# Hybrid attention block on one core: DMA additions to x moved behind the accumulations of weights, and the last additions written ahead of the rows

## The chip, the core and the metric

The kernel runs on one core of a Trainium2 chip. The metric is the device time of one execution in microseconds (us). Before the change three executions took 796.5, 797.93 and 798.8 us; the median, 797.93 us, is what a changed kernel is compared with.

## What is computed

One layer, float32, on 512 rows of 2048 numbers: a normalised sliding-window attention with 32 query and 4 key heads whose output is gated and multiplied by `w_out`, then a gated addition of an embedding, then a last normalisation.

```python
hn = rmsnorm(x, norm_g)
x = x + swa_mixer(hn, w_in, w_out, sinks, rel_bias)
emb = p @ ple_proj
g = sigmoid(rmsnorm(x, ple_norm) @ ple_gate)
x = x + emb * g
return rmsnorm(x, final_g)
```

The change lies in the last three lines.

## The kernel before, in words

**Products.** Every float32 matrix is split into a high part (a rounded copy, made by ACT, L755 or L763) and a low part (the rest, made by DVE, L756 or L764), and a product is three matmuls (`mm3`, L123). The big products by `w_out` and `ple_gate` follow a scheme with seven products of quarter matrices in place of eight, one level of it again for some of them. The products are numbered 1, 7, 6, 5, 3, 4 (`ORDER_PLE`). Each number p has two halves jj = 0, 1 of 512 columns; such a half is called the unit (p, jj) here. `unit` (L992) takes four pieces of weights, m = 0 to 3, and each piece, written (p, jj, m), is 128x1024 numbers (512 KB) and feeds 12 matmuls. Product 4 of the second matrix is no unit: it is done at the end in four blocks (`block`, L1568; jj, row block tb): (0,0), (1,0), (0,1) and (1,1), the last of them cut into a lower and an upper part.

**Weights.** `Pieces` (L720) hands them out. `get` of a piece first makes the loads and the splits that are due: a piece is split two pieces ahead of its use and loaded four raw pieces ahead. Loads go out on SP's queue (L747). Raw tiles (`braw`) have four buffers, so that a load waits for the split of the piece four before; the high and low tiles have three, so that a split waits for the matmuls of the piece three before. For products 7, 6 and 4 the weights are one sum that grows in place: loaded once for 7 (`grown`), then 6's and 4's share is added to it by an accumulating DMA on POOL's queue (L734), which must wait until the split for the product before has read the tile. There are eight such accumulations for 6 and eight for 4. The eight pieces of product 4 are split by `split_last(k)` (L759) at the steps that `early` (L1468) names, k = 7 at the very end.

**Gated additions.** `gated` (L1381) adds e * sigmoid(product) to one 128x512 tile of x, in steps: a sigmoid (ACT, L1387), a product with e (DVE, L1389) and the addition itself, then the square with its sum for the last normalisation (ACT, L1404). The addition is an accumulating DMA on POOL's queue (L1391, 256 KB) where rows and columns are both in the first or both in the second half, and a DVE instruction (L1393) elsewhere. Called "sum", for the first quarter of x (rows 0 to 255, columns 0 to 1023), there are four such DMAs; product 5 has four, for the last quarter; product 3 and the blocks of 4 use DVE.

**The order written out.** From the second product of `ORDER_PLE` on nothing is scheduled by a planner: each engine runs its instructions in the order in which the program writes them. `later` is a list of steps, and after each piece `some_later(4 - m)` (L987) runs a share of it so that it is empty by the last piece of a unit; then `todo` (L1513) makes loads of e (L1371), a step of the next product's left operands (`fh` on ACT and `fl` on DVE, L865 and L866), `split_last`, `open_bank` (L1473) and `by_gain` (L1413, multiplication of a finished tile by `final_g`). `gate_later` (L1455) puts the steps of a gate in front of `later`. For "sum" and for product 5 it keeps the squares apart in `moved`; they are put on `later` at the end of the units (5,0) and (5,1), and what is left over is run among the blocks. The loads of e are SP instructions in the same order.

**The end.** After the units, `power_of_mean` (L1355) makes the factor of the last normalisation, `row` (L1419) and ACT multiplications make the finished rows, `store` (L1416) writes them, for rows 0 to 255 first (`rows_out`, L1424), then 256 to 383, then the last.

Of the kernel before, what the change touches and what calls it, by code (L numbers as in the profile page):

```python
# [55 lines left out]
def trunk_kernel(ctx: ExitStack, tc: tile.TileContext, a: dict):  # L56
# [101 lines left out]
    def run(gen):  # L158
        for _ in gen:
            pass  # L160
# [21 lines left out]
    kinds, g = [], 0  # L182
# [16 lines left out]
    for k in range(KC):  # L199
# [95 lines left out]
        if 3 <= k < 3 + NB:  # L295
            t = k - 3
# [384 lines left out]
    def block(nm, r, c, jj, m):  # L681

        r = r if nm == "w_out" else 3 - r
        return a[nm][2 * (c - 1) + jj, 4 * (r - 1) + m]
# [16 lines left out]
    for nm, p in SUMS:  # L701
        for q in (6, 5) if (nm, p) == ("ple_gate", 5) else (p,):
            sum_small(nm, q)
        for jj in range(2):
            for m in range(4):
                t = summed[nm, p, jj, m] = tc.dram_tile([P, WE], F32, name=f"{nm}_{p}_{jj}_{m}")
# [278 lines left out]
    later = []  # L985
# [369 lines left out]
    def power_of_mean(out, ssq, nm):  # L1355

        w = out.shape[-1]
        ms = const.tile([P, NB], F32, tag="ms_r", name=f"ms_{nm}")[:, :w]
        nc.vector.tensor_scalar(ms, ssq, 1.0 / D, EPS, op0=ALU.mult, op1=ALU.add)
        yield  # L1360
        nc.gpsimd.tensor_tensor(out, ms, power[:, :w], op=ALU.pow)
# [7 lines left out]
    def load_embeds(c, jj):  # L1369
        t = embed_of[c, jj] = late.tile([P, 2, 512], F32, tag="e", name=f"e{c}_{jj}", bufs=2)  # L1370
        nc.sync.dma_start(t, embeds[c, jj])  # L1371
# [9 lines left out]
    def gated(t, j, zin, z, e, c=slice(0, 512), share=1.0):  # L1381


        n = done[t]
        done[t] += 1
        xt = x1[j][:, t, c]
        nc.scalar.activation(z, zin, AF.Sigmoid, scale=rstd2[:, t : t + 1])  # L1387
        yield
        nc.vector.tensor_mul(z, e[:, c], z)  # L1389
        if (t >= 2) == (j >= 2):  # L1390
            nc.gpsimd.dma_start(xt, z, accum_op=ALU.add)  # L1391
        else:
            nc.vector.tensor_add(xt, xt, z)  # L1393
        yield
        if (t, j) == (3, 1) and share != 1.0:
            flat = x1s.rearrange("p j t c -> p (j t c)")
            at = (NB + 3) * 512
            xt = flat[:, at + c.start : at + c.stop + 1]
            nc.vector.scalar_tensor_tensor(
                out=s2[:, 1, 1, c.start - 1 : c.stop], in0=xt, scalar=share, in1=xt, op0=ALU.mult, op1=ALU.mult,  # L1400
                accum_out=ssq3[:, t, n : n + 1],
            )
        elif (t, j) != (3, 1):
            nc.scalar.activation(z, xt, AF.Square, accum_out=ssq3[:, t, n : n + 1])  # L1404
        else:
            nc.vector.scalar_tensor_tensor(
                out=z, in0=xt, scalar=share, in1=xt, op0=ALU.mult, op1=ALU.mult, accum_out=ssq3[:, t, n : n + 1]
            )

    def gain(j):  # L1410
        return fg[:, j * 512 : (j + 1) * 512]

    def by_gain(t, j):  # L1413
        nc.vector.tensor_mul(x1[j][:, t, :], x1[j][:, t, :], gain(j))

    def store(t, j):  # L1416
        nc.sync.dma_start(a["out"][t * P : (t + 1) * P, j * 512 : (j + 1) * 512], x1[j][:, t, :])

    def row(t, j, yn):  # L1419

        xt = x1[j][:, t, :]
        nc.vector.scalar_tensor_tensor(out=xt, in0=xt, scalar=yn, in1=gain(j), op0=ALU.mult, op1=ALU.mult)

    def rows_out(t):  # L1424

        for j in (2, 3):
            row(t, j, yn2[:, t : t + 1])
            store(t, j)
        for j in range(2):
            nc.scalar.mul(x1[j][:, t, :], x1[j][:, t, :], yn2[:, t : t + 1])  # L1430
            store(t, j)
# [3 lines left out]
    def gate(p, jj, ps, e):  # L1435

        zs = []
        for tb in range(2):
            v1, v2, v7 = s1[:, jj, tb], s2[:, jj, tb], s7[:, jj, tb]
            if p == 1:  # L1440
                nc.scalar.mul(v1, ps[tb], -1.0)
            elif p == 7:
                (nc.vector.tensor_copy if tb else nc.scalar.copy)(v7, ps[tb])
            elif p == 6:
                nc.vector.tensor_add(v2, ps[tb], v7)
            elif p == 5:
                nc.vector.tensor_add(v7, ps[tb], v7)
                zs.append((2 + tb, 2 + jj, v7, v7))
            elif p == 3:
                zs.append((tb, 2 + jj, ps[tb], v1))  # L1450
            else:
                zs.append((tb, jj, v1, v1))
        return [gated(*z, e[z[0]]) for z in zs]

    def gate_later(*v):  # L1455
        zs = gate(*v)
        steps = [[partial_of(next, z, None) for z in zs] for _ in range(3)]
        if v[0] in (5, "sum"):
            moved.append(steps.pop())
        later[:0] = [step for of in steps for step in of]  # L1460


    moved = []

# [11 lines left out]
    opens = {  # L1478
        (3, 1, 0): (0, 0, "t"), (3, 1, 1): (1, 0, "t"), (3, 1, 2): (0, 1, "o"), (3, 1, 3): (1, 1, "o", lower),
    }  # L1480
    gains = {(3, 0, 1): (0, 0), (3, 0, 2): (1, 0), (3, 1, 0): (0, 1), (3, 1, 2): (1, 1)}

    def split_last(k):
        if k % 2 == 0:
# [16 lines left out]
    for n, p in enumerate(ORDER_PLE[:-1]):  # L1501
        if n == 1:

            ctx.enter_context(
                tc.manual_schedule(
                    engines={getattr(mybir.EngineType, v) for v in ("PE", "SP", "DVE", "Activation", "Pool")}
                )
            )
        nxt = ple_forms.steps(ORDER_PLE[n + 1])
        for jj in range(2):  # L1510
            calls = iter(range(4))

            def todo():  # L1513
                step = next(calls)
                k = early.get((p, jj, step))
                if (p, jj, step) in embed_loads:
                    load_embeds(*embed_loads[p, jj, step])
                while small_due:
                    small_due.pop(0)()
                if turns:  # L1520
                    turn(*turns.pop(0), "t")
                    if not turns:
                        nc.vector.tensor_reduce(ss2, ssq2, axis=AX.X, op=ALU.add)
                        run(power_of_mean(rstd2, ss2, "r2"))
                        nc.scalar.activation(ss2[:, :1], ss2[:, :1], AF.Sigmoid)
                    return
                next(nxt, None)
                if p == 1:
                    next(nxt, None)
                if k is not None:  # L1530
                    split_last(k)
                if (p, jj, step) in opens:
                    open_bank(*opens[p, jj, step])
                if (p, jj, step) in gains:
                    by_gain(*gains[p, jj, step])

            def between(m, ps):
                if (p, m) == (7, 3):
                    gate(p, jj, ps, None)
                q = ple_steps.get((p, jj, m))  # L1540
                if q is not None:
                    small_ple.prepare(q)
                for q in SMALL["ple_gate"].get((p, jj), {}).get(m, ()):
                    small_ple.product(q)
                if (p, jj, m) == (6, 1, 1):
                    later.append(partial_of(gate_later, "sum", 0, None, embeds_for(1, 0)))

            ps = unit(p, jj, at_ple, ple_forms, todo, between)
            last_two, held_e = (p, jj) == (3, 1), {}
            if not (p == 7 or last_two):  # L1550
                later.insert(0, partial_of(gate_later, p, jj, ps, held_e))
            for of, which in EMBEDS.get((p, jj), ()):
                e = embeds_for(of, which)
                held_e.update(e)
                if of == 1:
                    later.insert(1, partial_of(gate_later, "sum", which, None, dict(e)))
                    held_e.clear()
            if p == 5:
                while moved:
                    later.extend(moved.pop(0))  # L1560
        run(nxt)
# [34 lines left out]
    next(root)  # L1596
    g = block(0, 0)
    run(root)
    for step in moved.pop():
        step()  # L1600
    next(g)
    rows_out(0)
    next(g)
    run(g)
    rows_out(1)
    g = block(1, 0)
    next(g)
    for j in (2, 3):
        by_gain(2, j)
    next(g)  # L1610
    run(g)
    for j in (2, 3):
        by_gain(3, j)
    nc.vector.tensor_reduce(ssum[:, 2:], ssq3[:, 2, :4], axis=AX.X, op=ALU.add)
    root = power_of_mean(yn2[:, 2:], ssum[:, 2:], "r4")
    next(root)
    g = block(0, 1)
    run(root)
    next(g)
    for j in range(2):  # L1620
        row(2, j, yn2[:, 2:])
        store(2, j)
    for j in (2, 3):
        nc.scalar.mul(x1[j][:, 2, :], x1[j][:, 2, :], yn2[:, 2:])
        store(2, j)
    next(g)
    run(g)

    base, yn = (const.tile([P, 1], F32, name=f"{v}_3") for v in ("base", "yn"))
    g = block(1, 1, lower)  # L1630
    next(g)
    by_gain(3, 0)
    next(g)
    run(g)
    n = done[3]
# [81 lines left out]
```

## Time and profile before

| | |
|---|---|
| three executions | 796.5, 797.93, 798.8 us |
| profiled execution, its own time | 798.63 us |
| its span, first to last instruction | 796.9 us |
| PE, DVE, ACT busy | 781.4 (98%), 613.9 (77%), 525.6 us (66%) |
| mean granted TensorE clock | 0.993 |
| accumulations of `ple_gate` weights from 640 us on (L734) | 16 of 512 KB |
| additions to x by DMA (L1391) | 8 of 256 KB |

PE is TensorE's matmuls, PEld its weight loads, DVE VectorE, ACT ScalarE, POOL GpSimd, SP the queue that issues most DMAs. A row of a timeline has the start, the duration, the engine, the line, the operation, what is written and read, and in brackets the idle time ahead of it with what ended that. Three executions that differ by 2.3 us set what can be told apart.

### The profile page before, as it was taken

How to read it: one execution, taken by the hardware profiler on the slowest of the kernel's cores; microseconds unless marked ns; L12 is line 12 of the kernel's file. 1: busy time of each engine (PE TensorE's matmuls, PEld its weight loads, DVE VectorE, ACT ScalarE, POOL GpSimd, SP SyncE). 2: the span in 40 equal slices, each digit the busy share in tenths (PEclk: the TensorE clock that was granted, in tenths of full speed). 3: DMA queues.
4: the chain of work that ended last, by engine and by line, in shares of the span. 5: the costliest groups of instructions: out<-in, count | busy, mean ns of one | idle time of the engine just before them, and what ended most of it. 6: DMA issues, size and time to landing. Idle time of an engine off the chain costs nothing. (4 is left out here: it accounts for less than half of the span.)

```text
span 796.9 us, 11160 instructions
## 1 busy us (share of the span) xinstructions
PE 781.4 (98%) x3708; PEld 650.7 (82%) x3708; DVE 613.9 (77%) x1054; ACT 525.6 (66%) x1103; POOL 147.0 (18%) x270
## 2 busy tenths in 40 slices
PE   9999999999999999999999999999999999999895
PEld 8888888888888888888888888888888888886684
DVE  4537697877878697777767998877897769897696
ACT  6733577665866677666766745667778966655773
POOL 0201423141322223141322100110000002122000
PEclk9999999999999999999999999999999999999898
DMA  9978999999999989998998499766894499979835
GB/s 341 293 200 295 208 276 296 288 290 253 284 285 272 250 241 295 249 313 233 298 253 186 160 345 350 230 210 241 313 357 173 151 338 276 269 208 272 263 100 182
DMA packets 49961, 205.94 MB, mean 258 GB/s; under 512 B 7456, under 2 KB 8480, under 8 KB 44144
## 3 DMA queue, kind: packets, MB, share of 16 engines
q1 hardware_dynamic: 39152, 154.58, 55.4%
q0 software_dynamic: 10752, 50.66, 31.3%
q8 instruction: 29, 0.48, 0.2%
q14 instruction: 28, 0.23, 0.1%
HBM read 192.31 MB, written 75.55 MB: 336 GB/s over the span
## 5 line engine op out<-in xcount | busy, mean ns | idle before, releaser
L756 DVE TENSOR_TENSOR blo<-braw,bhi 128x1024 fp32r<-128x1024 f32 x100 | 122.0, 1223 | 38.4 <-ACT bhi L755 37.6
L755 ACT CAST bhi<-braw 128x1024 fp32r<-128x1024 f32 x100 | 104.9, 1050 | 45.2 <-PE o L128 17.1
L126 PE MATMUL gps<-xh,whi 128*128 128x512 f32 x256 | 100.0, 390 | 0.0
L127 PE MATMUL gps<-xl,whi 128*128 128x512 f32 x256 | 99.9, 390 | 0.0
L128 PE MATMUL gps<-xh,wlo 128*128 128x512 f32 x256 | 99.7, 390 | 0.0
L126 PE MATMUL qps<-xh,whi 128*128 128x512 f32 x224 | 87.8, 392 | 0.0
L127 PE MATMUL qps<-xl,whi 128*128 128x512 f32 x224 | 87.4, 390 | 0.0
L128 PE MATMUL qps<-xh,wlo 128*128 128x512 f32 x224 | 87.3, 390 | 0.0
L570 POOL TENSOR_SCALAR_AFFINE_SELECT own<-r 64x512 fp32r<-64x512 f32 (+1 forms) x48 | 32.5, 677 | 243.3 <-DVE r L560 243.3
L110 DVE TENSOR_TENSOR wlo<-wraw,whi 128x1024 fp32r<-128x1024 f32 x60 | 73.5, 1227 | 2.8 <-ACT whi L109 2.7
L127 PE MATMUL o<-blo,fho 128*128 128x512 f32 x192 | 74.9, 390 | 0.0
L126 PE MATMUL o<-bhi,fho 128*128 128x512 f32 x192 | 74.8, 390 | 0.0
L128 PE MATMUL o<-bhi,flo 128*128 128x512 f32 x192 | 74.8, 389 | 0.0
L556 ACT CAST r<-pt 128x256 fp32r<-128x256 f32 x64 | 23.9, 374 | 68.7 <-PE pt L551 68.5
L126 PE MATMUL g<-bhi,fhg 128*128 128x512 f32 x160 | 64.3, 402 | 2.6 <-ACT bhi L755 2.6
L127 PE MATMUL g<-blo,fhg 128*128 128x512 f32 x160 | 64.4, 402 | 2.1 <-DVE blo L756 2.1
L109 ACT CAST whi<-wraw 128x1024 fp32r<-128x1024 f32 x60 | 62.3, 1040 | 4.6 <-issue 4.1
L128 PE MATMUL g<-bhi,flg 128*128 128x512 f32 x160 | 63.4, 396 | 0.0
L128 PEld LDWEIGHTS gps<-xh,wlo 128*128 128x128 f32 x256 | 48.1, 188 | 10.3
L126 PEld LDWEIGHTS gps<-xh,whi 128*128 128x128 f32 x256 | 48.1, 188 | 9.2
L529 ACT ACTIVATE t<-t,sm 128x129 f32<-128x129 f32 (+1 forms) x128 | 49.6, 389 | 8.8 <-DVE sm L525 7.3
L560 DVE TENSOR_TENSOR r<-pt,r 128x256 fp32r<-128x256 f32 x56 | 23.7, 424 | 41.0 <-ACT r L556 40.3
(290 smaller groups left out, 1835.7 us busy)
## 6 DMA issues: line engine op xcount, KB each, us to landing
wraw<-in_w_gate_in SPq DMA_DIRECT2D x32, 512.0 KB, 8.2
w_out<-in_w_out POOLq DMA_DIRECT2D x32, 512.0 KB, 9.1
braw<-w_out SPq DMA_DIRECT2D x32, 512.0 KB, 5.5
wraw<-in_w_q SPq DMA_DIRECT2D x28, 512.0 KB, 6.5
braw<-in_w_out SPq DMA_DIRECT2D x22, 512.0 KB, 4.7
braw<-in_ple_gate SPq DMA_DIRECT2D x22, 512.0 KB, 8.3
xw<-in_first SPq DMA_DIRECT2D x14, 640.5 KB, 6.7
w_out<-in_w_out SPq DMA_DIRECT2D x16, 512.0 KB, 10.5
```

The source lines that it names most:

```text
L109: nc.scalar.copy(hi, raw)
L110: nc.vector.tensor_sub(lo, raw, hi.bitcast(F32))
L126: nc.tensor.matmul(ps, sh, mh, start=first, stop=False, skip_group_check=more)
L127: nc.tensor.matmul(ps, sh, ml, start=False, stop=False, skip_group_check=more)
L128: nc.tensor.matmul(ps, sl, mh, start=False, stop=last, skip_group_check=more)
L529: nc.scalar.activation(su, su, AF.Exp, bias=sm[:, u : u + 1], accum_out=sm[:, 2 + u : 3 + u])
L556: nc.scalar.copy(rh, src)
L560: nc.vector.tensor_sub(rl, src, rh.bitcast(F32))
L570: nc.gpsimd.affine_select(out=flat(own), in_=flat(r).bitcast(F32), pattern=[[0, 8], [sign, HB]], compare_op=ALU.is_ge, fill=0.0, base=-HB ...
L755: nc.scalar.copy(hi[:, :n], raw)
L756: nc.vector.tensor_sub(lo[:, :n], raw, hi[:, :n].bitcast(F32))
```

## The change

In `gated` the addition by DMA becomes a step of its own for rows 0 to 255. `gate_later` takes the four additions of "sum" out of `later` and keeps them in `moves`; they are put on `later` at the end of unit (5,0), so that they run within unit (5,1). The squares in `moved` follow one unit later than before: at the end of (5,1) and of (3,0). The four `by_gain` of the first quarter are spread over unit (3,1). At the end, each block's product and addition stand ahead of the finished rows that stood ahead of them, and block (0,1) comes behind the rows 256 to 383.

```diff
         nc.vector.tensor_mul(z, e[:, c], z)
         if (t >= 2) == (j >= 2):
+            if t < 2:
+                yield
             nc.gpsimd.dma_start(xt, z, accum_op=ALU.add)
...
-        steps = [[partial_of(next, z, None) for z in zs] for _ in range(3)]
+        steps = [[partial_of(next, z, None) for z in zs] for _ in range(4 if v[0] == "sum" else 3)]
         if v[0] in (5, "sum"):
             moved.append(steps.pop())
+        if v[0] == "sum":
+            moves.extend(steps.pop())
         later[:0] = [step for of in steps for step in of]
...
-    gains = {(3, 0, 1): (0, 0), (3, 0, 2): (1, 0), (3, 1, 0): (0, 1), (3, 1, 2): (1, 1)}
+    gains = {(3, 1, 0): (0, 0), (3, 1, 1): (1, 0), (3, 1, 2): (0, 1), (3, 1, 3): (1, 1)}
...
-            if p == 5:
+            if (p, jj) == (5, 0):
+                later.extend(moves)
+            elif (p, jj) in ((5, 1), (3, 0)):
                 while moved:
                     later.extend(moved.pop(0))
...
     g = block(0, 0)
     run(root)
-    for step in moved.pop():
-        step()
+    next(g)
     next(g)
     rows_out(0)
-    next(g)
     run(g)
-    rows_out(1)
     g = block(1, 0)
     next(g)
+    next(g)
+    rows_out(1)
     for j in (2, 3):
         by_gain(2, j)
-    next(g)
     run(g)
-    for j in (2, 3):
-        by_gain(3, j)
     nc.vector.tensor_reduce(ssum[:, 2:], ssq3[:, 2, :4], axis=AX.X, op=ALU.add)
     root = power_of_mean(yn2[:, 2:], ssum[:, 2:], "r4")
     next(root)
-    g = block(0, 1)
     run(root)
-    next(g)
     for j in range(2):
         row(2, j, yn2[:, 2:])
         store(2, j)
     for j in (2, 3):
         nc.scalar.mul(x1[j][:, 2, :], x1[j][:, 2, :], yn2[:, 2:])
         store(2, j)
+    g = block(0, 1)
     next(g)
+    next(g)
+    for j in (2, 3):
+        by_gain(3, j)
     run(g)
+    by_gain(3, 0)
 
     base, yn = (const.tile([P, 1], F32, name=f"{v}_3") for v in ("base", "yn"))
     g = block(1, 1, lower)
     next(g)
-    by_gain(3, 0)
     next(g)
     run(g)
```

More of the change, by code (lines that the diff above doesn't have):

```diff
@@ L1456, in gate_later @@
         zs = gate(*v)
-        steps = [[partial_of(next, z, None) for z in zs] for _ in range(3)]
+        steps = [[partial_of(next, z, None) for z in zs] for _ in range(4 if v[0] == "sum" else 3)]
         if v[0] in (5, "sum"):
             moved.append(steps.pop())
+        if v[0] == "sum":
+            moves.extend(steps.pop())
         later[:0] = [step for of in steps for step in of]
-    moved = []
+    moved, moves = [], []
     rooms4 = {}
```

## The prediction

> **What bounds the kernel now.** I read the page first, then the windows of the stretch in which the change works, then the timelines of PE, ACT, POOL and DVE there.
>
> ```profile
> PE 781.4 (98%) x3708; PEld 650.7 (82%) x3708; DVE 613.9 (77%) x1054; ACT 525.6 (66%) x1103; POOL 147.0 (18%) x270
> 700.00:705.00 5.00, 5.00 (x24) 4.14 (x23) 5.00 (x7) 3.54 (x5) 0.00 (x0) 1.00 0.63 233
> 705.00:710.00 5.00, 5.00 (x24) 4.14 (x23) 3.51 (x4) 2.95 (x4) 0.00 (x0) 1.00 0.35 108
> 725.00:730.00 5.00, 4.24 (x18) 2.98 (x17) 2.37 (x3) 1.55 (x2) 1.03 (x2) 1.00 1.05 278
> 745.00:750.00 5.00, 4.66 (x11) 3.73 (x12) 5.00 (x8) 4.89 (x8) 0.00 (x0) 0.50 0.74 303
> ```
>
> The columns of a window are its length, then PE, PEld, DVE, ACT and POOL busy with their counts, the granted clock, the DMA share and GB/s. PE is the bound (98%), and yet it stands still between 725 and 750, where the DMA engines are full (1.05), while at 705 to 710 they are at 0.35.
>
> ```profile
> 711.20 0.39 PE L126 MATMUL g<-bhi,fhg 128*128 128x512 f32 x1
> 722.08 0.39 PE L126 MATMUL g<-bhi,fhg 128*128 128x512 f32 x1
> 744.08 0.70 PE L126 MATMUL g<-bhi,fhg 128*128 128x512 f32 x1 [2.62 <-ACT bhi L755]
> 745.34 0.80 PE L127 MATMUL g<-blo,fhg 128*128 128x512 f32 x1 [0.56 <-DVE blo L756]
> 764.83 0.39 PE L126 MATMUL open<-last,fhg 128*128 128x512 f32 x1
> ...
> 726.55 1.05 ACT L755 CAST bhi<-braw 128x1024 fp32r<-128x1024 f32 x1 [5.60 <-DMA braw<-ple_gate]
> 742.99 1.04 ACT L755 CAST bhi<-braw 128x1024 fp32r<-128x1024 f32 x1 [5.10 <-DMA braw<-in_ple_gate]
> ```
>
> Unit (5,0) starts at 711.20 and (5,1) at 722.08: an undisturbed unit takes 10.88 us, a piece 2.72. Block (0,0) starts at 764.83. Between stand four units, 43.5 us, in 53.63 us: **10.1 us are lost**. They go to pieces that came late by DMA: (5,1,2), cast at 726.55, and (3,0,2), cast at 742.99. The latter also leaves the clock at half (0.50 at 745 to 750).
>
> [...]
>
> Why were the DMA engines idle and then full?
>
> ```profile
> 690.93 0.87 POOL L734 DMA_DIRECT2D grown<-in_ple_gate  x1 [3.01 <-DVE blo L756]
> 710.79 1.79 POOL L1391 DMA_DIRECT2D x1s<-s  x2 [18.99 <-DVE s L1389]
> 711.94 3.34 POOL L734 DMA_DIRECT2D grown<-in_ple_gate  x3
> 723.36 1.77 POOL L1391 DMA_DIRECT2D x1s<-s  x2 [8.08 <-DVE s L1389]
> 724.51 1.52 POOL L734 DMA_DIRECT2D grown<-in_ple_gate  x1
> 733.84 1.76 POOL L1391 DMA_DIRECT2D x1s<-s  x2 [7.80 <-DVE s L1389]
> ...
> 693.45 1.23 DVE L756 TENSOR_TENSOR blo<-grown,bhi 128x1024 fp32r<-128x1024 f32 x1
> 704.46 1.22 DVE L756 TENSOR_TENSOR blo<-grown,bhi 128x1024 fp32r<-128x1024 f32 x1
> ...
> L734 POOL DMA_DIRECT2D grown<-in_ple_gate x3: 1544/1897/2244, 711.9 to 713.0; - x3
> DMA to landing us min/median/max: 10.2/13.5/16.8
> ```
>
> POOL waits 18.99 us for the product of the first "sum" addition, and behind that stand accumulations whose tiles were read by 694.7 (693.45 + 1.23) to 705.7. Three go out together at 711.9 to 713.0, the fourth behind the next two additions, at 724.5. The three land 3.85 us apart ((713.0 + 16.8 - 711.9 - 10.2) / 2) beside SP's loads, which get as late.
>
> **The change, part by part.** No instruction is added or removed: four additions, their squares and the products by `final_g` are the same in number, all is order.
>
> *The accumulations* go out at 694.7 to 705.7, as their tiles come free. The DMA engines have room there (0.63 and 0.35). The twelfth, out at 690.93, should land near 700.2; four more and the four loads of unit (5,0) beside them at 3.85 us a pair are down by 715.6. Piece (5,0,3) is needed at 711.20 + 3 x 2.72 = 719.4 less a cast (1.05) and a subtraction (1.22), at 717.1: 1.5 us to spare. So the cost is nothing, hidden by matmuls of (5,0); a load late by more would cost PE that. Loads for (5,1) then have the engines to themselves, and the 10.1 us should go. Unit (3,0) starts at 711.20 + 2 x 10.88 = 732.96.
>
> *What is late next.* Unit (3,0) and after it are where ACT and DVE are full, and they give the end. Their chain starts with the cast of (3,0,2).
>
> ```profile
> 728.77 1.28 DVE L1447 TENSOR_TENSOR s<-g,s 128x512 f32<-128x512 f32 x2
> 744.06 1.23 DVE L756 TENSOR_TENSOR blo<-braw,bhi 128x1024 fp32r<-128x1024 f32 x1 [6.15 <-ACT bhi L755]
> 745.20 1.28 DVE L1447 TENSOR_TENSOR s<-g,s 128x512 f32<-128x512 f32 x2
> 771.45 1.22 DVE L764 TENSOR_TENSOR low<-grown,last 128x1024 fp32r<-128x1024 f32 x1
> 788.99 0.38 DVE L1389 TENSOR_TENSOR s<-e,s 128x224 f32<-128x224 f32 x1
> ...
> 729.49 0.73 ACT L1387 ACTIVATE s<-s,rstd 128x512 f32<-128x512 f32 x1 [1.89 <-DVE s L1447]
> 743.94 0.61 ACT L865 CAST fhg<-hT 128x512 fp32r<-128x512 f32 x1
> 744.46 1.04 ACT L763 CAST last<-grown 128x1024 fp32r<-128x1024 f32 x1
> 745.61 1.04 ACT L755 CAST bhi<-braw 128x1024 fp32r<-128x1024 f32 x1
> 746.56 1.33 ACT L1387 ACTIVATE s<-s,rstd 128x512 f32<-128x512 f32 x2
> 751.67 0.63 ACT L1404 ACTIVATE s<-x1s 128x512 f32<-128x512 f32 x1
> 752.30 0.62 ACT L1404 ACTIVATE s<-x1s 128x512 f32<-128x512 f32 x1
> ```
>
> Before, that cast is at 742.99, the last split (`split_last(7)`) ends at 772.6 (771.45 + 1.22), and the last product of a gate, which starts the final steps, is at 788.99. With no stall the cast needs only the end of unit (5,1), whose matmuls free its tile: 733.2, **9.8 us earlier**. Then is added to the chain:
>
> (a) The squares of "sum", from (5,1) into (3,0), between casts: 4 x 0.63 (752.30 - 751.67) = 2.5 us.
> (b) The squares of (5,1) come from the end into (3,1,3), ahead of the casts of `split_last(6)` and (7): 2 x 0.63 = 1.3 us.
> (c) With six squares on `later` (3,0)'s first `some_later` takes two items of seven, not one of three, so the first sigmoid of (5,1) now stands ahead of `fh` and `split_last(0)`. It waits for L1447, which stands behind the subtraction: 745.20 + 0.72 (729.49 against 728.77 of its releaser) is 2.9 us after the cast's start at 742.99; ACT, free after 0.95 (746.56 - 745.61, cast to next), waits 2.0 us. Behind it wait `fh` and two casts, and DVE for these.
> (d) ACT waits for the additions to land that it squares.
>
> ```profile
> 723.33 1.22 DVE L853 TENSOR_TENSOR hT<-hT,hT 128x1024 f32<-128x1024 f32 x1
> 727.63 1.23 DVE L756 TENSOR_TENSOR blo<-braw,bhi 128x1024 fp32r<-128x1024 f32 x1 [3.08 <-ACT bhi L755]
> ...
> L1391 POOL DMA_DIRECT2D x1s<-s x2: 870/1026/1182, 710.8 to 711.4; - x2
> DMA to landing us min/median/max: 4.1/5.2/6.4
> ...
> L1391 POOL DMA_DIRECT2D x1s<-s x2: 865/1011/1157, 733.8 to 734.4; - x2
> DMA to landing us min/median/max: 8.9/9.9/10.9
> ```
>
> In `later` the additions of product 5's first half come first (the gate is put in front), so POOL issues **six in a row**. From the subtraction of (5,1,2) to the first of them is 733.84 - 727.63 = 6.2 us. That subtraction can follow L853, done at 724.6, so I take 724.9: issue from 731.1, the first landing 4.1 us later, at 735.2 (the row of 710.8, little else under way). The others land 2.6 us apart when loads run beside them (734.4 + 10.9 - 733.8 - 8.9). Bounds of the spacing: nothing but the issue (six in some 3.5 us, so 0.6), and the 3.85 us of the heavier accumulations; I take 2.2, near the row of the same DMA, since SP's loads leave gaps. The fifth lands at 744.0. ACT gets to its square after the cast of (3,0,2), the wait (c), and two sigmoids, two `fh`, three casts and two squares, at 0.6 (1.33 for two, overlapping), 0.5 (744.46 - 743.94), 0.95 and 0.63: 733.2 + 0.95 + 2.0 + 1.2 + 1.0 + 2.85 + 1.3 = 742.5. So it waits 1.5 us, 0 at best, 8.1 at worst (3.85: 750.6).
>
> The `by_gain` only move inside the chain: zero, at worst 2 x 0.69 on DVE. SP's loads of e and weights keep their order; they are merely earlier. POOL's queue past (5,1): the additions of (5,1) stand behind the six, but their squares come a whole unit later.
>
> *The end.* With (b) gone from there, ACT reaches the sigmoid of block (0,0) 1.3 us earlier, but the block's DVE work behind it waits for the factor too; following the order through I find 0.4 us gained (bounds 0 and 1.3). Products ahead of rows put block (0,1) behind row 2 and two `by_gain` on its path, which before stood beside a wait: in these 0.4.
>
> **Sum**: -9.8 + 2.5 + 1.3 + 2.0 + 1.5 - 0.4 = **-2.9 us**. PE is then no longer the bound there: it will stop a little for (3,1,1), (3,1,2) and `split_last(7)`, and gets back 10.1 us less these. The profiled execution took 798.63 us with a span of 796.9; 2.9 less gives 794.0 of span. Against the median, 797.93, it gives 795.0.
>
> **Rivals.**
>
> *ACT is ahead of DVE and hides its waits* (791.5): (c) and (d) cost nothing, and -2.9 - 3.5 = -6.4. For it: DVE, not ACT, is the later one in (3,0) before. Against: ACT is busy for 4.89 of 5 us at 745 to 750 already, and gets the four squares besides.
>
> *PE alone bounds* (787.8): all 10.1 us. Against it DVE's 5.00 of 5.00 at 745 to 750 and on.
>
> *Nothing comes of it* (797.5): the traffic moves from one full stretch to another; the accumulations catch (5,0,3) late, or each addition takes 2.6 us and the sixth holds ACT once more, some 2.5 us together. For it: the landings of 10.2 to 16.8 us.
>
> *Slower* (801): ACT, in order, stands before the square in (3,0,2) until the six additions land. From a landing of the fifth after 746.9 (2.9 us past 744.0) the time is above before, us for us. At the accumulations' 3.85 us apart it lands at 750.6: +6.6 - 2.9 = +3.7, 801.6; PE would stand for over 3 us and, as at 744, fall to half rate. For it: four loads beside the six (three weights and an e). Against: 256 KB is half an accumulation.
>
> That the change does not do what it says I count out by the order: no accumulation is due after (5,1,0).
>
> **How the numbers follow.** Forecast 0.45 (own range 793 to 797), -6.4 us 0.17, PE alone 0.06, nothing 0.15, slower 0.17. The range leaves out PE alone and the upper part of slower: 790.5 to 800. 0.3% (2.4 us) is about what a measurement tells from no change. Faster than 795.5: 0.23 and 0.30 of the forecast's 0.45, 0.53; within: 0.15 and 0.15, 0.30; slower: 0.17.
>
> **What would show it.** L734's last four issues at 695 to 706, with no 19 us gap; no DMA-ended idle time on ACT at 720 to 735; unit (3,0) starting near 733; POOL with six L1391 in a row near 731; ACT idle in (3,0,2), ended by a DMA on x1s; `split_last(7)` ending near 770. Wrong if PE stalls in (5,0), or if PE runs through (3,1) without stops.

## The result, and the profile after

After the change the median of 19 executions is 799.71 us (798.34 to 800.47), beside 798.01 us (796.5 to 799.13) for 19 executions of the kernel before: a ratio of 1.0023 (95% interval 1.0016 to 1.003). The change makes the kernel slower by a little, 0.23%, where 795.0 us had been forecast. The profiled execution of after took 799.52 us, with a span of 797.8 us; its span is 0.9 us above that of before, and the rest of the 1.7 us between the medians is that the profiled execution of before lay 0.6 us above its median and that of after 0.2 us below.

The first part of the forecast came true. The windows of after, for three of the stretches shown of before and two more (length; PE, PEld, DVE, ACT, POOL busy; clock; DMA share; GB/s):

```profile
705.00:710.00 5.00, 5.00 (x24) 4.14 (x23) 3.50 (x4) 2.90 (x5) 0.87 (x1) 1.00 1.06 265
725.00:730.00 5.00, 5.00 (x24) 4.14 (x23) 4.03 (x6) 3.07 (x5) 0.00 (x0) 1.00 0.79 271
745.00:750.00 5.00, 2.05 (x10) 1.35 (x8) 1.01 (x2) 3.16 (x7) 0.00 (x0) 1.00 1.08 302
750.00:755.00 5.00, 3.40 (x8) 2.51 (x9) 3.81 (x4) 5.00 (x11) 0.00 (x0) 0.62 0.56 146
755.00:760.00 5.00, 5.00 (x18) 3.97 (x17) 4.96 (x7) 4.86 (x7) 0.00 (x0) 0.70 0.00 0
```

The DMA engines are now busy from 705 to 710, where they stood at 0.35, and PE no longer stops at 725 to 730. But from 745 to 750 PE and DVE stand still for most of the time while the DMA engines are full, and after that PE's granted clock is 0.62 and 0.70 (0.50 in the windows of 2 us from 752 to 758). POOL's timeline shows why both are so:

```profile
694.87 0.87 POOL L734 DMA_DIRECT2D grown<-in_ple_gate  x1 [3.17 <-DVE blo L756]
699.47 0.88 POOL L734 DMA_DIRECT2D grown<-in_ple_gate  x1 [3.74 <-DVE blo L756]
703.54 0.88 POOL L734 DMA_DIRECT2D grown<-in_ple_gate  x1 [3.19 <-DVE blo L756]
705.87 0.87 POOL L734 DMA_DIRECT2D grown<-in_ple_gate  x1 [1.46 <-DVE blo L756]
731.54 5.33 POOL L1393 DMA_DIRECT2D x1s<-s  x6 [24.80 <-DVE s L1389]
```

The accumulations go out one by one, each as soon as its tile has been read (L756). Then POOL does nothing for 24.80 us, and six additions go out in a row (L1393 is the line of the addition now; L1406 the square, L1449 what L1447 was). ACT's timeline, from the end of unit (5,0) on:

```profile
712.02 1.05 ACT L755 CAST bhi<-braw 128x1024 fp32r<-128x1024 f32 x1 [1.03 <-DMA braw<-ple_gate]
715.83 1.05 ACT L755 CAST bhi<-braw 128x1024 fp32r<-128x1024 f32 x1 [2.76 <-DMA braw<-ple_gate]
...
733.25 1.05 ACT L755 CAST bhi<-braw 128x1024 fp32r<-128x1024 f32 x1 [1.11 <-PE g L128]
736.23 0.72 ACT L1387 ACTIVATE s<-s,rstd 128x512 f32<-128x512 f32 x1 [1.93 <-DVE s L1449]
...
742.26 0.63 ACT L1406 ACTIVATE s<-x1s 128x512 f32<-128x512 f32 x1 [0.82 <-DMA x1s<-s]
744.92 0.63 ACT L1406 ACTIVATE s<-x1s 128x512 f32<-128x512 f32 x1 [1.93 <-DMA x1s<-s]
747.48 0.63 ACT L1406 ACTIVATE s<-x1s 128x512 f32<-128x512 f32 x1 [1.84 <-DMA x1s<-s]
748.11 0.60 ACT L865 CAST fhg<-hT 128x512 fp32r<-128x512 f32 x1
...
749.56 1.04 ACT L755 CAST bhi<-braw 128x1024 fp32r<-128x1024 f32 x1
```

The cast of (3,0,2) waits for no DMA any more; it stands at 733.25 in place of 742.99, 9.74 us earlier. Nine microseconds later ACT stands three times, 0.82, 1.93 and 1.84 us, before a square whose tile has not landed. Behind it wait `fh` (748.11), the high part of `split_last` (748.61) and the cast of (3,1,1) (749.56), although the trace shows nothing that these wait for but their place in the queue. DVE waits for that `fh`, and PE for the cast:

```profile
748.74 0.69 DVE L866 TENSOR_TENSOR flg<-hT,fhg 128x512 fp32r<-128x512 f32 x1 [5.00 <-ACT fhg L865]
772.40 1.22 DVE L764 TENSOR_TENSOR low<-grown,last 128x1024 fp32r<-128x1024 f32 x1
789.83 0.38 DVE L1389 TENSOR_TENSOR s<-e,s 128x224 f32<-128x224 f32 x1
```

```profile
750.65 0.50 PE L126 MATMUL g<-bhi,fhg 128*128 128x512 f32 x1 [3.61 <-ACT bhi L755]
```

The last split ends at 773.62 (772.40 + 1.22), 0.95 us behind before's 772.67; what follows it up to the last product of a gate takes 16.2 us (789.83 - 773.62) against 16.3. So all of the span's 0.9 us arises ahead of the last split.

### The profile page after: what moved, and what is told of

Its sections match the earlier page's. It is cut to its first block, busy times and chain, and to the rows that moved or that the text cites. A ratio compares the mean times of both kernels' runs of the same rounds, so it can differ in the third digit from the quotient of the medians.

```text
span 797.8 us, 11160 instructions
## 1 busy us (share of the span) xinstructions
PE 780.2 (98%) x3708; PEld 651.0 (82%) x3708; DVE 613.8 (77%) x1054; ACT 525.5 (66%) x1103; POOL 147.3 (18%) x270
## 5 line engine op out<-in xcount | busy, mean ns | idle before, releaser
L756 DVE TENSOR_TENSOR blo<-braw,bhi 128x1024 fp32r<-128x1024 f32 x100 | 121.7, 1221 | 29.7 <-ACT bhi L755 29.0
```

Source lines behind the costliest of these rows:

```text
L756: nc.vector.tensor_sub(lo[:, :n], raw, hi[:, :n].bitcast(F32))
```

## The experiments

The theory after the result: the late issue of the additions of "sum" puts six of them in one row beside SP's loads, and **ACT's 4.6 us before their squares** turn a gain into a loss. The rivals: the steps that were moved onto ACT, the squares and the first sigmoid of (5,1), cost more than thought; or the new order of the end does. All ratios are to the kernel before, with 95% intervals; its median stood at 798.25 us beside the first four kernels, at 798.35 beside the next three that were run together (e5, e6, e7) and at 798.36 beside e8 and e9.

### e1: the four additions of "sum" issued as soon as POOL is free

From after; the squares stay where the change put them, and four empty steps keep the shares of `some_later`.

```diff
                 k = early.get((p, jj, step))
+                if (p, jj, step) == (5, 1, 0):
+                    while moves:
+                        moves.pop(0)()
...
             if (p, jj) == (5, 0):
-                later.extend(moves)
+                later.extend([lambda: None] * 4)
```

> The four additions of "sum" go out at step (5,1,0), ahead of product 5's two and still behind all accumulations; four empty steps take their places on the list, so that ACT and DVE keep the order of the changed kernel. Theory (ACT waits for the landing of six additions in a row): the idle times of 0.82, 1.93 and 1.84 us that end with a DMA on x1s go from ACT, PE no longer stands 3.6 us near 750 nor falls to half clock, the last split ends some 4 us earlier; 799.7 - 4 = 795.7 us, faster than before (798.0). Rival 1 (it is the place of the six squares among the casts that costs, wherever the additions land): nothing changes, 799.7. Rival 2 (the new order of the end costs): nothing changes, 799.7.

795.71 us, 0.9969 (0.9957 to 0.9981): 4.0 us below after. POOL's timeline and then ACT's, of e1 (its trace runs about 1 us behind that of after from 700 us on, ahead of any edit):

```profile
711.66 1.76 POOL L1393 DMA_DIRECT2D x1s<-s  x2 [3.95 <-DVE s L1389]
725.12 1.76 POOL L1393 DMA_DIRECT2D x1s<-s  x2 [11.70 <-DVE s L1389]
732.43 1.75 POOL L1393 DMA_DIRECT2D x1s<-s  x2 [5.55 <-DVE s L1389]
```

```profile
734.91 1.05 ACT L755 CAST bhi<-braw 128x1024 fp32r<-128x1024 f32 x1 [1.60 <-DMA braw<-in_ple_gate]
...
742.99 0.62 ACT L1406 ACTIVATE s<-x1s 128x512 f32<-128x512 f32 x1
```

The six go out in three pairs, all of them behind the last accumulation (706.84), and no square waits for a landing: the three stand back to back (742.99, 743.61, 744.22). Four of ACT's 4.6 us come back as time. PE's longest stop ahead of 770 is 0.95 us there, in place of 3.61. The rivals do not explain that, since all that they name is still in e1.

### e4: before, with the new order of the end alone

```diff
     next(g)
+    next(g)
     rows_out(0)
-    next(g)
     run(g)
-    rows_out(1)
     g = block(1, 0)
     next(g)
+    next(g)
+    rows_out(1)
     for j in (2, 3):
         by_gain(2, j)
-    next(g)
     run(g)
-    for j in (2, 3):
-        by_gain(3, j)
...
-    g = block(0, 1)
     run(root)
-    next(g)
...
+    g = block(0, 1)
     next(g)
+    next(g)
+    for j in (2, 3):
+        by_gain(3, j)
     run(g)
+    by_gain(3, 0)
...
-    by_gain(3, 0)
...
```

> The kernel before with nothing but the new order from the last gate on (products and additions ahead of the rows, block (0,1) behind the rows 256 to 383). Theory: the end's order is worth 0 to -0.4 us: 797.6 to 798.0. Rival 2 (the end's order costs what the change lost): 799.7.

798.4 us, 0.9999 (0.999 to 1.0008). DVE's timeline of e4, last split and last product of a gate:

```profile
769.27 1.22 DVE L764 TENSOR_TENSOR low<-grown,last 128x1024 fp32r<-128x1024 f32 x1
786.78 0.38 DVE L1389 TENSOR_TENSOR s<-e,s 128x224 f32<-128x224 f32 x1
```

From the end of the one to the start of the other 16.29 us (786.78 - 770.49), and 16.32 before. (That execution took 796.41 us, 2 us less than its median, so its times of day are not to be compared, only the stretch.) The end neither gains nor costs: that rival falls, and with it the 0.4 us that the prediction put down as a gain.

### e2 and e3: what the moved squares cost

e2 is e1 with the lists of `moved` put on `later` two squares to a step at the end of (5,1), so that `some_later` takes one item less early in (3,0). e3 is e2 with the squares of (5,1) back at the end, where they stand before.

```diff
+    def both(steps):
+        for step in steps:
+            step()
...
-            elif (p, jj) in ((5, 1), (3, 0)):
+            elif (p, jj) == (5, 1):
+                while moved:
+                    later.append(partial_of(both, moved.pop(0)))
+            elif (p, jj) == (3, 0):
                 while moved:
                     later.extend(moved.pop(0))
```

> As the one before, and the squares that come to unit (3,0) are three steps of two, so that the first step of (3,0) is the gate alone and the first sigmoid of (5,1) stands behind fh and split_last(0) again. Theory: the 1.9 us that ACT waits for DVE there was a term of its own on the chain and goes: 795.7 - 1.9 = 793.8. Rival 1 (DVE is behind anyway and hides that wait): 795.7, no change.

```diff
-            elif (p, jj) == (3, 0):
-                while moved:
-                    later.extend(moved.pop(0))
...
     run(root)
+    for step in moved.pop():
+        step()
     next(g)
```

> As the one before, and the two squares of (5,1) are back at the end, out of (3,1,3). Theory: the casts of split_last(6) and (7) come 1.3 us earlier and the end with them: 793.8 - 1.3 = 792.5. Rival: the squares only change place, since in the end ACT and DVE wait for each other in a chain as long: 793.8.

e2: 795.25 us, 0.9968 (0.9955 to 0.998), half a microsecond below e1 and no more. It tells little of (c), because the pairs also put a fourth square into (3,0,3); e8 below does it cleanly. e3: 793.0 us, 0.9941 (0.9928 to 0.9953), 2.2 us below e2 where 1.3 had been expected. The last split, on DVE's timelines of e2 and then of e3:

```profile
768.20 1.22 DVE L764 TENSOR_TENSOR low<-grown,last 128x1024 fp32r<-128x1024 f32 x1
```

```profile
765.19 1.22 DVE L764 TENSOR_TENSOR low<-grown,last 128x1024 fp32r<-128x1024 f32 x1
```

In these two executions it stands 3.0 us earlier (2.2 by the medians). DVE waited 0.87 us for ACT ahead of the split before the last in e2, and not at all there in e3: a square costs more there than its own 0.63 us, for it also makes DVE wait. Part of that is the order which the squares bring with them. With them on the list `some_later` runs three steps of the gate at a time where it ran two, so that in e2 the two additions of the gate of (3,0) fall into different groups of steps: on DVE they start at 755.61 and 758.68, with a split and a `by_gain` between them, and ACT waits 2.34 us before the second square (759.40). In e3 they start at 757.04 and 758.37, and ACT waits 1.26 and 0.60 us before the two squares.

### e8: the first sigmoid of (5,1) behind `fh` again

e1 with one empty step ahead of the gate, so that unit (3,0) begins in the order of before. The idle time of (c) goes; the question is whether time goes with it.

```diff
                 later.insert(0, partial_of(gate_later, p, jj, ps, held_e))
+                if (p, jj) == (5, 1):
+                    later.insert(0, lambda: None)
```

> As the first experiment, with one empty step ahead of the gate of (5,1), so that the first step of (3,0) runs the gate alone and the first sigmoid stands behind fh and split_last(0); unlike the second experiment every square keeps its place. Theory: the 1.9 us wait of ACT was a term of its own: 795.7 - 1.9 = 793.8 us. Rival (what the second experiment suggests: DVE is the later one there and hides it): 0.5 us at most, 795.2.

795.98 us, 0.9961 (0.9949 to 0.9974): the same as e1. ACT's timeline of e8:

```profile
737.68 1.06 ACT L755 CAST bhi<-braw 128x1024 fp32r<-128x1024 f32 x1 [0.40 <-PE g L128]
...
741.80 1.06 ACT L755 CAST bhi<-braw 128x1024 fp32r<-128x1024 f32 x1 [1.32 <-DMA braw<-in_ple_gate]
742.77 0.62 ACT L1406 ACTIVATE s<-x1s 128x512 f32<-128x512 f32 x1
```

The wait for L1449 is gone and ACT is earlier by it, only to stand 0.40 us for PE and 1.32 us for the load of (3,1,0). The first square starts at 742.77, with 742.99 in e1. So a stall of about 2 us was really there, as (c) said, and taking it away gives nothing, because PE and the next piece of weights together hold ACT nearly as long (1.72 us).

### e5 and e9: the two halves of the change alone

e5 is before with the order of POOL's DMAs alone: the additions of "sum" held apart, but issued at step (5,1,0) as in e1. Squares, `by_gain` and the end stay as before. e9 is the rest alone: after with the additions back at their old place.

```diff
         if (t >= 2) == (j >= 2):
+            if t < 2:
+                yield
             nc.gpsimd.dma_start(xt, z, accum_op=ALU.add)
...
+        steps = [[partial_of(next, z, None) for z in zs] for _ in range(4 if v[0] == "sum" else 3)]
         if v[0] in (5, "sum"):
             moved.append(steps.pop())
+        if v[0] == "sum":
+            moves.extend(steps.pop())
...
+                if (p, jj, step) == (5, 1, 0):
+                    while moves:
+                        moves.pop(0)()
```

> The kernel before with one thing changed: the four additions of "sum" go out at step (5,1,0), behind all accumulations; squares, by_gain and the end stay as before. Theory: the accumulations go out at 695 to 706, the 10.1 us of stops go, and the chain of ACT and DVE has nothing added but a wait of some 2 us in (5,1,3) for the landing of the last of the four (734.4 in the third experiment): its first cast is near 735.5 in place of 743.0, 7.5 us earlier, 790.8 us. Rival (the gain of the third experiment needs the squares in (3,0) and the by_gain in (3,1)): no better than there, 793.0 or above.

791.23 us, 0.9914 (0.9901 to 0.9927): 7.1 us below before, and the best of all kernels here. POOL's, ACT's and DVE's timelines of e5:

```profile
711.02 1.77 POOL L1393 DMA_DIRECT2D x1s<-s  x2 [3.95 <-DVE s L1389]
725.34 1.76 POOL L1393 DMA_DIRECT2D x1s<-s  x2 [12.55 <-PE g L128]
732.65 1.76 POOL L1393 DMA_DIRECT2D x1s<-s  x2 [5.56 <-DVE s L1389]
```

```profile
735.89 1.04 ACT L755 CAST bhi<-braw 128x1024 fp32r<-128x1024 f32 x1
```

```profile
764.34 1.22 DVE L764 TENSOR_TENSOR low<-grown,last 128x1024 fp32r<-128x1024 f32 x1
```

The cast of (3,0,2) is 7.1 us earlier than before (735.89, 742.99), the last split too (764.34, 771.45), and so is the time; all additions stand behind the last accumulation (706.21). The gain is not the whole 9.74 us of after's cast: ahead of the cast stand the four squares of "sum", from 732.48 on, with one cast among them and no idle time. None waits for a landing, where a wait of some 2 us had been expected; the forecast of the cast (735.5) came near by luck, for the squares' own time (four of 0.62 us) is about as long.

e9, the other half:

```diff
         if (t >= 2) == (j >= 2):
-            if t < 2:
-                yield
             nc.gpsimd.dma_start(xt, z, accum_op=ALU.add)
...
             if (p, jj) == (5, 0):
-                later.extend(moves)
+                later.extend([lambda: None] * 4)
```

> The changed kernel with the four additions of "sum" back in their old place, each behind its product, ahead of the accumulations; squares, by_gain and end stay as changed. Theory: the stops of 10.1 us stay as before, and the chain behind them has the squares of "sum" (2.5 us) and of (5,1) (2.2 us by the third experiment) in addition, with no wait for landing: 798.3 + 4.7 = 803.0 us. Rival (what stands in (3,0) is covered by the stops for DMA): 798.3, as before.

803.97 us, 1.0066 (1.0053 to 1.008): 5.6 us above before. ACT's and DVE's timelines of e9:

```profile
742.65 1.05 ACT L755 CAST bhi<-braw 128x1024 fp32r<-128x1024 f32 x1 [5.67 <-DMA braw<-in_ple_gate]
```

```profile
776.88 1.22 DVE L764 TENSOR_TENSOR low<-grown,last 128x1024 fp32r<-128x1024 f32 x1
```

The cast of (3,0,2) is as late as before, and the last split 5.4 us later: this is what the moved steps add when nothing is gained ahead of them. The halves together would give -7.1 + 5.6 = -1.5 us. e1, which has both with the additions early, has -2.5; after has +1.7. So 3 to 4 us of after belong to neither half: they come of the additions being so late while their squares stand in (3,0).

### e6 and e7: the landings themselves

e6 meant to keep the six in a row but with those of "sum" ahead, by running these just ahead of product 5's in the program.

```diff
+        if v[:2] == (5, 0):
+            steps[1] = [partial_of(sum_first, step) for step in steps[1]]
...
+    def sum_first(step):
+        while moves:
+            moves.pop(0)()
+        step()
...
-                later.extend(moves)
+                later.extend([lambda: None] * 4)
```

> The changed kernel, six additions in a row at the same time, but those of "sum" ahead of product 5's. Theory (each square waits for the landing of its own addition): with landings at about 735, 740, 742, 745, 747.5 and 750 the squares of "sum" hardly wait, ACT waits 1.5 to 2 us each for product 5's two in (3,0,3), the cast of (3,1,2) is at 752.3 in place of 753.8: 799.7 - 1.5 = 798.2 us. Rival (it is the number of DMAs and squares there, not which lands first): 799.7.

795.91 us, 0.9972 (0.9962 to 0.9982), near no expectation, since its premise failed. POOL's timeline of e6:

```profile
724.35 1.76 POOL L1393 DMA_DIRECT2D x1s<-s  x2 [11.55 <-DVE s L1389]
```

The place in the program is no time: nothing stood in POOL's queue ahead of them, so they went out when POOL came free and their products were made, as in e1 (the first pair at 711.03). In after they stood behind product 5's, and these wait for a product that DVE makes behind its subtraction of (5,1,2). e6 thus repeats e1, and says nothing on the order of landings.

e7 halves what is moved: in after, each addition of "sum" takes 64 of its 128 partitions, so that half of the first quarter of x goes without the addition.

```diff
-            nc.gpsimd.dma_start(xt, z, accum_op=ALU.add)
+                nc.gpsimd.dma_start(xt[:64], z[:64], accum_op=ALU.add)
+            else:
+                nc.gpsimd.dma_start(xt, z, accum_op=ALU.add)
```

> The changed kernel with half of each "sum" addition: 64 of 128 partitions are added, the other half of the first quarter of x goes without. Theory (landings are paced by the bytes, or descriptors, that each addition shares the engines with): the four land 1.3 us apart, ACT waits about 1 us in all in place of 4.6: 799.7 - 3.6 = 796.1 us. Rival (each addition takes its turn with a whole load of SP, whatever its size): still 2.6 us apart, 799.7.

796.81 us, 0.9981 (0.9972 to 0.9989), 2.9 us below after with issue, order and number of instructions the same. The line of the additions in e7, then in after (the six of 731 us):

```profile
L1393 POOL DMA_DIRECT2D x1s<-s x4: 1482/1934/2410, 732.1 to 733.7; - x4
...
  ACT s L1408: 0.5, 1
...
DMA to landing us min/median/max: 8.1/9.5/10.8
```

```profile
L1393 POOL DMA_DIRECT2D x1s<-s x6: 867/1676/2536, 731.5 to 734.3; - x6
...
  ACT s L1406: 4.6, 3
...
DMA to landing us min/median/max: 3.8/10.6/15.8
```

In after the first lands at 735.35 (731.54 + 3.81) and the sixth at 750.1 (734.3 + 15.8); in e7 the four halves land from 740.3 to 744.5, and ACT waits 0.5 us in place of 4.6. What the additions move decides ACT's wait, as the theory says; whether it is the bytes or the partitions, both halved in e7, this run does not tell apart. The profiled execution of e7, 795.16 us, is the fastest of its twelve (median 796.81), so the waits hold for that one, and the 2.9 us are those of the medians.

## Why the prediction was wrong, step by step

**Right.** The accumulations cost nothing and the stops of PE at 711 to 745 go: (5,0,2) and (5,0,3) were cast 1.03 and 2.76 us late, under matmuls. Unit (3,0) began as forecast: cast at 733.25 (733.2 said), -9.74 us (-9.8). The six in a row began at 731.54 (731.1), and the first landed at 735.35 (735.2). The squares took 0.63 us each as in (a), and the wait of (c) was 1.93 us (2.0). So was the mechanism of the rival *slower* and its threshold: above a landing of the fifth at 746.9 the time was to exceed before's, and it landed at 747.45 (the square behind it starts at 747.48).

**The step that failed is (d)**, in the spacing of the landings: "I take 2.2, near the row of the same DMA, since SP's loads leave gaps." They left none. From SP's queue in after, loads of weights and then of e:

```profile
L747 SPq DMA_DIRECT2D braw<-in_ple_gate x3: 328/328/1758, 733.3 to 736.1; - x3
...
DMA to landing us min/median/max: 6.7/8.1/11.7
...
L1371 SPq DMA_DIRECT2D e<-embeds x1: 1119/1119/1119, 734.9 to 734.9; - x1
...
DMA to landing us min/median/max: 10.4/10.4/10.4
```

Three loads of weights, and one of e between them, went out within 3 us and were under way up to 747.8 (736.1 + 11.7), so that from the first landing on an addition shared the DMA engines with a load all the time: their share stands at 1.06 to 1.08 in every 5 us from 735 to 750. The first gap between landings was 4.3 us (735.35 to 739.6), more than the 3.85 us that the prediction took as its upper bound; the others were 2.6 each (ACT's squares start at 742.26, 744.92, 747.48). The fifth landed 3.4 us later than said, 2.1 of them by the first gap and 1.2 by the three others, and ACT stood 4.6 us in place of 1.5. With 2.6 for every gap, (d) would have been 3.1 us (745.6 - 742.5) and the forecast 796.6. So the choice of 2.2 accounts for about half of what (d) was short of, and the first gap, for which no row of before gave a price, for the rest.

The 2.6 can be worked out: an addition of 256 KB and a load of 512 KB are 786,432 bytes, and at the 302 GB/s of the window at 745 that is 2.6 us. The rows of before gave nearly the same price (2.6 us apart, and 278 GB/s in the full window at 725, by which the two take 2.8 us), and the prediction bent it downward for gaps that it did not show. That an addition took as long there as a load of twice its bytes is seen in the packets: from 742.3 to 744.9 after's DMA view counts 144 packets (0.26 MB, one addition) on POOL's queue and 144 (0.52 MB, one load) on SP's. The landings agree: each of an addition (739.6, 742.3, 744.9, 747.5) is followed 0.3 to 0.4 us later by one of a load (740.0, 742.6, 745.3, 747.8). The first gap does not come out this way. From 735.4 to 739.6 the two queues moved 0.39 and 0.70 MB at 264 GB/s, more than one addition (0.26 MB) and one load (0.52 MB), and yet of the additions only the second landed, at the end of that time; why stays open.

**How the sum comes out.** The last split was to come 2.5 us earlier than before (-2.9, of which 0.4 at the end) and came 0.95 later: 3.45 us off. Of that (d) has 3.1 (4.6 - 1.5). The remaining 0.35 holds errors that went both ways: (b) is worth 2.2 us by e3, not 1.3; (c) is there, but its 2.0 us are right by luck: without it ACT waits about as long for PE and a load (e8), a wait that the prediction did not have. At the end the 0.4 us gained were none (e4). So 3.1 of the 3.8 us between the forecast of the span (794.0) and the span (797.8) are (d), and e1, which takes ACT's waits away, gives 4.0 us back. By the prediction's other terms e1 would be at 793.5 (795.0 less 1.5); it is at 795.7. The end (0.4) and (b) (0.9) make 1.3 of these 2.2 us, and 0.7 the cast of (3,0,2), which waits 1.60 us for its load there (734.91, less the 1 us by which that trace is behind, against 733.25). That these add up is argued, not shown. That the half clock of PE (0.50) from 752 to 758 costs something of its own in after is likewise only argued: no run held the stop and took the slow clock away.

The rival *ACT is ahead of DVE* had (c) and (d) cost nothing. It fell with (d), for ACT's waits before the squares are what decided; taking (c) away does gain nothing, but not because DVE hides it. *PE alone bounds* would need the squares, too, to cost nothing, and e9 shows them to cost 5.6 us together with the new places of the sigmoid and of the `by_gain`. *Nothing comes of it* named the right price, "each addition takes 2.6 us", and then let it hold ACT for 2.5 us only. It did not have the first gap of 4.3 us.

## What to carry to other kernels

An addition whose product comes late can hold what stands behind it in its queue: in before POOL sat idle for 18.99 us ahead of one, and the accumulation behind it, whose tile had been read by 694.7, went out at 711.9. Moving the additions back was worth 7.1 us (e5). But move them only as far as the queue is free, not as far as one can: in after they went out from 731.54 on, and ACT stood 4.6 us before the squares that read their results, with a cast behind them (749.56) for which the trace shows no other wait; e1, which issues them earlier, is 4.0 us faster. Price a row of DMAs by the bytes of all queues that are busy then, divided by the GB/s of a window that is full, and follow the landings to the instruction that reads them; here that gives the later gaps (2.6 us), while the first (4.3 us) was longer. Follow-up work that is moved into a stretch where the engines are full anyway (ACT 4.89 and DVE 5.00 of 5 us from 745 to 750 in before) is better left where it was: six squares of 0.63 us (3.8 us in all), with the new places of the sigmoid and of the `by_gain`, cost 5.6 us here (e9).

## What the runs showed of the hardware

In after, PE's stop of 3.61 us, with another of 0.95 us behind it, was followed by a granted clock of 0.50 in each window of 2 us from 752 to 758, with 5.9 us of PE's busy time, and by 0.99 in the next. In e1 a stop of 1.89 us was followed by 0.56 and 0.59, and by 1.00 from 775 on. PE's timeline of e1 and its windows of 2 us:

```profile
770.42 0.50 PE L127 MATMUL open<-low,fhg 128*128 128x512 f32 x1 [1.89 <-DVE low L764]
```

```profile
771.00:773.00 2.00, 2.00 (x7) 1.56 (x6) 1.97 (x4) 1.04 (x2) 0.93 (x1) 0.56 0.09 35
773.00:775.00 2.00, 2.00 (x7) 1.56 (x6) 0.88 (x2) 2.00 (x6) 0.00 (x0) 0.59 0.71 254
775.00:777.00 2.00, 2.00 (x11) 1.64 (x10) 1.97 (x4) 1.43 (x4) 0.00 (x0) 1.00 0.91 270
```

In e2 a stop of 1.91 us for the same split, ahead of 769.47, left the granted clock at 1.00 (windows of 5 us from 765 to 780). In e6 the stop for that split took 1.9 us, and the windows of 2 us from 769 on had 0.78, 0.50, 0.87 and 1.00. So a stop of about 1.9 us was followed by a lower clock in two of these three traces; what spared the third these runs do not show.
